# The last product in two column halves, one of the last multiplications on GpSimd, and the order and size of the last stores

## The chip, the cores and the metric

The kernel runs on one core of one Trainium2 chip. The metric is the device time of one execution in microseconds (us), as the median of several executions. A core has five engines that run side by side and wait for each other through semaphores: TensorE (PE in the profile, its weight loads PEld), VectorE (DVE), ScalarE (ACT), GpSimd (POOL) and SyncE (SP, which here only issues transfers). A "q" behind an engine's name in the profile means its sequencer, the part that issues its instructions, waits, branches and starts transfers.

## The reference

```
batch, m, k, n = 16, 512, 1024, 768
y1 = np.matmul(x, w1)          # x (16, 512, 1024), w1 and w2 (1024, 768)
y2 = np.matmul(x, w2)
return (np.tanh(y1) * y2).astype(np.float32)
```

So 8192 rows of x, in 64 row tiles of 128, are multiplied by two weight matrices, and every output element is the tanh of one product times the other product.

## The kernel before

**Tiling.** The 64 row tiles fall into a head of 4, computed with plain matmuls while the weights are still landing, and 20 triples of three row tiles (`i` from 0 to 19). The 2 x 768 weight columns are three blocks of 512: `a` is `w1[:, :512]`, `b` is `w2[:, :512]`, and `g` holds `w1[:, 512:]` in its first 256 columns and `w2[:, 512:]` in its last 256. The inner dimension of 1024 is two halves of four 128-row steps. For one triple this is a product of a 3 x 2 block matrix with a 2 x 3 block matrix, 18 block products; the kernel forms sums of blocks (`A_SUMS` on x, `B_SUMS` on the weights) and needs 15, `p0` to `p14`. Each is four matmuls of 128x128 by 128x512 that accumulate in one PSUM bank (`product`, L440 to L443).

**What goes around the products.** `C_OPS` lists, for one triple, the products and what combines them: `copy` and `seed` (ACT copies a bank to SBUF or into another bank), `add` (DVE adds or subtracts a bank and an SBUF tile), `t` and `th` (ACT's tanh, of 512 columns or of the 256 columns of `w1` in block `g`, into an output tile `o`), `m` and `mh` (DVE multiplies that output tile by the other product, in place, 512 or 256 columns wide). The number behind `t`, `th`, `m`, `mh` is the row tile of the triple. The entries that matter here, near the end of the list, are

```
("seed16", "seed", ("add52",), "c9", "c1", -1),
("p2", "p", ("seed16",), "c9", 4, 6, False),
("m1", "m", ("p2", "t1"), 1, "c9", 1),
("p3", "p", ("add52", "seed16"), "c1", 8, 48, False),
("add4", "add", ("copy56", "p3"), "c8", "c1", "s56", (-1, 1)),
("th0", "th", ("add4",), 0, "c8", 1),
("mh0", "mh", ("add4", "th0"), 0, "c8", 1),
("th1", "th", ("p3",), 1, "c1", 1),
("mh1", "mh", ("p3", "th1"), 1, "c1", 1),
```

`c0` to `c10` are PSUM banks. So `p3` completes bank `c1`, which both `add4` (DVE) and `th1` (ACT) read, and `p2` completes bank `c9`, which `m1` reads. Where two engines touch one PSUM bank, the framework puts a semaphore between them, in the order in which the program names them.

**Order.** A planner (class `Planner`) lays all operations out in advance: each has an engine, an estimated duration, a due time, what it needs, and what it must only stay behind. The products have a fixed order (`plan.strict`, from `PE_ORDER`, and for the last triple `LAST_ORDER = "0 13 4 5 3 2"`); everything else takes the free slot that the planner finds, by due time when it has a choice. The planned start times give one program order (`sorted`, a stable sort, so that equal starts keep the order of the list), and each engine's queue runs its share of it strictly in order. `LATENCY` in the planner is what it reckons from the end of an operation to its use on another engine.

**The end of the program.** One piece of the head is held back: block `g` of row tile 3, eight matmuls `m3g0` to `m3g7` on a kept copy of that tile (L426), which the planner puts into gaps of TensorE during the last triple. Their due time is 10000 and more, so that they, their tanh `thg3` (L429) and their multiplication `mug3` (L433) give way to everything else. The output tiles of the last triple are rows 61, 62 and 63; each is stored in two parts, columns 0 to 511 and 512 to 767, by SP (L423), in the order in which the planner finds them done. Behind the last operation every engine reads a flag (L734; it says whether the inputs were in the range that the fast path takes, and is complete some 19 us before the end), branches over the general path (L735), drains and meets the others in a barrier (L828), for which SP first waits for every transfer.

GpSimd starts the loads of x with a cast to fp16 (L358) and runs a tiny copy in front of most of them, which makes it wait for an earlier transpose (L479). Its last load is that of row tile 63.

Of the kernel before, what the change touches and what calls it, by code (L numbers as in the profile page):

```python
# [9 lines left out]
ALU = mybir.AluOpType  # L10
# [60 lines left out]
LAST_ORDER = "0 13 4 5 3 2"  # L71


class Planner:
# [9 lines left out]
    def op(self, name, engines, due, needs, fn, *args, behind=(), issued=(), chains=(), xfer=0.0, latency=None, seeds=False,  # L84
           lands=None, hold=0.0):
        assert name not in self.ops, name
        self.ops[name] = dict(engines=engines, due=due, needs=[n for n in needs if n], behind=[n for n in behind if n], issued=[n for n in issued if n], fn=fn, args=args,
                              chains=chains, xfer=xfer, latency=latency, seeds=seeds, lands=lands, hold=hold)
        for c in chains:
            self.chains.setdefault(c, {"left": 0, "bank": None, "end": 0.0})["left"] += 1  # L90
# [149 lines left out]
def kernel(  # L240
# [7 lines left out]
    nc = tc.nc  # L248
    P = 128
    B, M, K = x.shape  # L250
    _, N = w1.shape
    KO = K // P
    KH = KO // 2
    MT = B * M // P
    F = 512
    G = N - F
    HEAD = 4
    TRIPLES = (MT - HEAD) // 3
# [7 lines left out]
    bf16, f16, f32, i32 = mybir.dt.bfloat16, mybir.dt.float16, mybir.dt.float32, mybir.dt.int32  # L266
# [8 lines left out]
    once = fast.enter_context(tc.tile_pool(name="once", bufs=1))  # L275
# [13 lines left out]
    wsum = {v: once.tile([P, KH, F], f16, name=f"b{v}") for v, *_ in B_SUMS}  # L289

    S_NAMES = [o[3] for o in C_OPS if o[1] in ("copy", "add") and o[3][0] == "s"]
    arena = once.tile([P, len(S_NAMES) * C_BUFS * F], f32, name="arena")
    SLOTS = len(S_NAMES) * C_BUFS
    c_bufs = {(s, j): arena[:, (n * C_BUFS + j) * F:(n * C_BUFS + j + 1) * F]
# [19 lines left out]
    op = plan.op  # L314
# [87 lines left out]
    def w_rhs(v, k):  # L402
        return w_block(v, slice(k, k + 1))[:, 0, :]
# [6 lines left out]
    def x_operand(i, v):  # L410
        if v & (v - 1):
            return s_bufs[v, i % S_BUFS]
        bit = v.bit_length() - 1
        return xt(HEAD + 3 * i + bit // 2)[:, bit % 2 * KH:(bit % 2 + 1) * KH, :]
# [4 lines left out]
    def out_tile(mt):  # L419
        return o_bufs[mt if mt < HEAD else HEAD + (mt - HEAD) % O_BUFS]  # L420
# [14 lines left out]
    def place(i, name):  # L435
        if name[0] == "c":
            return bank((i, name))
        return c_bufs[name, i % C_BUFS]

    def product(e, i, dst, a, b, begins):  # L440
        for k in range(KH):
            pin(nc.tensor.matmul(place(i, dst), x_operand(i, a)[:, k, :], w_rhs(b, k),  # L442
                                 start=begins and k == 0, stop=k == KH - 1, skip_group_check=True))  # L443

    def c_copy(e, i, dst, src, sign):
# [12 lines left out]
    def c_mul(e, i, r, src, lo, n, at):  # L458
        o = out_tile(HEAD + 3 * i + r)[:, lo:lo + n]
        pin(nc.vector.tensor_tensor(o, o, place(i, src)[:, at:at + n], ALU.mult))  # L460

    def flag_1(e):
        pin(nc.vector.tensor_scalar(good, sums, HIGH, None, ALU.is_le))
# [33 lines left out]
        position["p" + p, TRIPLES - 1] = TRIPLES * 15 + n  # L497
    sequence = sorted((z, i, p) for (p, i), z in position.items())
    slot_of = {(i, p): ORIGIN + z * SLOT for z, i, p in sequence}
    plan.strict = [f"{p}.{i}" for _, i, p in sequence]  # L500

    XW, XX = 0.655, 1.4
    on_sp = "x00 x10 x20 x30 x01 x11 a4 a5 x21 a6 x31 a7".split() + [f"g{k}{t}" for k in range(KH) for t in range(2)]
# [60 lines left out]
    def plain(mt, s, due, behind=()):  # L564
        for n, k in enumerate([k for u, k in slices if u == s]):
            before = list(behind) + ([f"m{mt}{s}0"] if n else [])
            op(f"m{mt}{s}{k}", {"pe": MM}, due(n), [f"c{s}{k}", f"e{mt}{k // KH}"], mm, (s, mt), mt, k, w_cols(s, k), n == 0,
               behind=before, chains=[(s, mt)])
        last = [f"m{mt}{s}{k}" for k in range(KO)]
        xt_readers[mt] += last  # L570
        return last
# [6 lines left out]
    def finals(mt, s, due, last):  # L578
        if s != "b":
            lo, n = (0, F) if s == "a" else (F, G)  # L580
            op(f"th{s}{mt}", {"act": 0.5 if n == F else 0.28}, due, last, plain_tanh, mt, lo, n, (s, mt), 0,
               behind=reuse_out(mt), chains=[(s, mt)])
        if s != "a":
            lo, n, at = (0, F, 0) if s == "b" else (F, G, G)
            op(f"mu{s}{mt}", {"dve": 0.6 if n == F else 0.33}, due, last + [f"th{'a' if s == 'b' else s}{mt}"], plain_mul, mt, lo, n,
               (s, mt), at, chains=[(s, mt)])
            outs[mt].insert(0 if s == "b" else 1, f"mu{s}{mt}")

    for n, s in enumerate("agb"):
        for mt in range(HEAD):  # L590
            if (s, mt) == ("g", HEAD - 1):
                due, behind = (lambda n: 1e4 + n), [f"p0.{TRIPLES - 1}"]
            else:
                due, behind = (lambda n: landed[slices["agb".index(s) * KO + n]] + 0.8 + 0.02 * mt), []
            finals(mt, s, due(KO - 1) + (5.0, 3.0, 4.0)[n], plain(mt, s, due, behind))

    c_ops = {o[0]: o for o in C_OPS}
    readers = {}
# [40 lines left out]
    for i in range(TRIPLES):  # L639
        for name, kind, needs, *_ in C_OPS:  # L640
            soonest[i, name] = max([until[i, n] for n in needs] + ([slot_of[i, name]] if kind == "p" else []))
            until[i, name] = soonest[i, name] + TIME[kind] + 0.2
        for v, a, b, how in A_SUMS:
            op(f"S{v}.{i}", {"dve": 0.335}, None, x_needs(i, a) + x_needs(i, b), x_sum, i, v, a, b, how,
               hold=needed(i, v) - S_AHEAD if i > 1 else 0.0,
               behind=[f"{r}.{i - S_BUFS}" for r in a_readers[v]] if i >= S_BUFS else first_done)
            for u in (a, b):
                if not u & (u - 1):
                    xt_readers[HEAD + 3 * i + (u.bit_length() - 1) // 2].append(f"S{v}.{i}")
        for o in C_OPS:  # L650
            name, kind, needs = o[:3]
            needs = [f"{n}.{i}" for n in needs]
            chains = sorted({(i, p) for p in o[3:6] if isinstance(p, str) and p[0] == "c"})
            if kind == "p":
                needs += x_needs(i, o[4]) + w_needs(o[5], 0) + w_needs(o[5], 1)
                op(f"{name}.{i}", {"pe": SLOT}, slot_of[i, name], needs, product, i, *o[3:], chains=chains)
                if not o[4] & (o[4] - 1):
                    xt_readers[HEAD + 3 * i + (o[4].bit_length() - 1) // 2].append(f"{name}.{i}")
                continue
            if kind in ("seed", "copy", "add"):  # L660
                before = []
                if o[3][0] == "s":
                    before = [f"{r}.{i - C_BUFS}" for r in readers[o[3]]] if i >= C_BUFS else all_casts
                if kind == "add":
                    op(f"{name}.{i}", {"dve": 0.6}, None, needs, c_add, i, *o[3:], behind=before, chains=chains, seeds=True)
                else:
                    op(f"{name}.{i}", {"act": 0.495}, None, needs, c_copy, i, *o[3:], behind=before, chains=chains, seeds=True)
                continue
            r = o[3]
            mt = HEAD + 3 * i + r  # L670
            due = soonest[i, name] + LAST
            if kind in ("t", "th"):
                lo, n = (0, F) if kind == "t" else (F, G)
                op(f"{name}.{i}", {"act": 0.5 if n == F else 0.285}, due, needs, c_tanh, i, r, o[4], lo, n, o[5],
                   behind=reuse_out(mt), chains=chains)
            else:
                lo, n, at = (0, F, 0) if kind == "m" else (F, G, G)
                op(f"{name}.{i}", {"dve": 0.6 if n == F else 0.335}, due + 1, needs, c_mul, i, r, o[4], lo, n, at, chains=chains)
                outs[mt].insert(0 if kind == "m" else 1, f"{name}.{i}")
    for mt in range(MT):  # L680
        i = (mt - HEAD) // 3 if mt >= HEAD else -1
        if mt < HEAD:
            n = F if mt == HEAD - 1 else N
            op(f"st{mt}", {"sp": 0.05}, 1e3, outs[mt][:1] if mt == HEAD - 1 else outs[mt], store, mt, 0, n, behind=[f"p12.{4 + mt}"], xfer=1.0)
            if n < N:
                op(f"st{mt}M", {"sp": 0.05}, 2e4, outs[mt][1:], store, mt, n, N - n, xfer=0.4)
            continue
        late = [f"{('p0', 'p4', 'p12')[(mt - HEAD) % 3]}.{i + 1}"] if i < TRIPLES - 2 else []
        if i == TRIPLES - 1:
            for a, lo, n in ((0, 0, F), (1, F, G)):  # L690
                part = outs[mt][a:a + 1]
                op(f"st{mt}{a}", {"sp": 0.05}, 2e4, part, store, mt, lo, n, xfer=0.4)
        else:
            op(f"st{mt}", {"sp": 0.05}, slot_of[max(i, 0), "p2"] + 12, outs[mt], store, mt, behind=late, xfer=1.0)
# [138 lines left out]
```

## Time and profile before

| what | us |
|---|---|
| median of 3 runs (lowest, highest) | 303.63 (303.56, 304.0) |
| span of the profiled execution, first to last instruction | 303.7 |
| device time noted for the profiled execution, with what lies around the span | 305.48 |
| TensorE busy | 291.2 (96%) |
| VectorE busy | 254.0 (84%) |
| ScalarE busy | 224.5 (74%) |
| GpSimd busy | 49.6 (16%) |
| last matmul ends | 298.1 |
| last VectorE instruction ends | 299.65 |
| last store: issued, landed | 299.77, 302.56 |

The span counts from the first to the last instruction of the program. Times of instructions are given from the start of the span. In the timeline a row is one instruction or several alike in a row (x3): its start, its length, the engine, the line of the kernel, the operation, what it writes and reads; in brackets how long the engine stood idle before it, and what ended that. Back-to-back instructions of one engine overlap a little, so that a row of three is shorter than three times one.

### The profile page before, as it was taken

The numbers are of one execution on the slowest core, as the hardware profiler recorded it, in microseconds if no ns is written. First come the engines' busy times: TensorE is split into PE (matmuls) and PEld (weight loads), VectorE is DVE, ScalarE is ACT, GpSimd is POOL, SyncE is SP. The second block draws the span as 40 slices with busy tenths as digits, with TensorE's granted clock in tenths as the row PEclk, the third lists the DMA queues.
The fourth block names the chain that finished last, engine by engine and source line by source line (L and its number), as shares of the span: only waits on it lengthen the run. The fifth ranks groups of instructions, "written<-read, shape, count | busy, mean of one in ns | idle before, by whom it ended". The sixth has DMA issues, their size and how long they took to land.

```text
span 303.7 us, 4640 instructions
## 1 busy us (share of the span) xinstructions
PE 291.2 (96%) x1377; PEld 133.3 (44%) x1377; DVE 254.0 (84%) x530; ACT 224.5 (74%) x451; POOL 49.6 (16%) x128
## 2 busy tenths in 40 slices
PE   8989989999999999999998999999999999999992
PEld 5435434444444444444443444444444444444440
DVE  1639999999797898978959898898989889898773
ACT  2687897688877988789787888767787767776542
POOL 0054032130301210212112111211121210000000
PEclk9999999999999999999999999999999999999999
DMA  7999999999999999999999999999999999131242
GB/s 232 385 290 208 169 124 144 175 203 236 187 158 222 190 276 281 154 205 277 210 225 241 238 245 230 249 254 190 254 280 164 299 246 253 77 155 52 104 190 92
DMA packets 84283, 63.51 MB, mean 209 GB/s; under 512 B 62752, under 2 KB 66336, under 8 KB 84256
## 3 DMA queue, kind: packets, MB, share of 16 engines
q1 hardware_dynamic: 73888, 45.36, 63.1%
q0 software_dynamic: 9792, 16.78, 38.2%
q10 hardware_dynamic: 576, 1.05, 1.0%
q8 instruction: 11, 0.18, 0.2%
q14 instruction: 16, 0.13, 0.2%
HBM read 39.85 MB, written 25.17 MB: 214 GB/s over the span
## 4 chain that ended last, share of the span: by engine, by line
PE 59%; DMA 26%; DVE 8%; ACT 2%; issue 2%; SPq 1%; ACTq 0%; POOL 0%; DVEq 0%; POOLq 0%
PE bank L442 55%; DMA xT<-xh 13%; DMA xh<-in_x_dram 7%; DMA arena<-in_w_dram 4%; PE bank L426 3%; DVE bank L452 3%; DVE o L460 2%; DVE early_x L417 2%; DMA wh<-in_w_dram 2%; ACT o L455 1%; ACT junk L386 1%; DVE arena L452 1%; PE bank L376 0%; ACTq L353 0%; DVE b L408 0%
## 5 line engine op out<-in xcount | busy, mean ns | idle before, releaser
L442 PE MATMUL bank<-b,early_x 128*128 128x512 f16 x640 | 148.4, 379 | 0.8 <-DVE arena L452 0.4
L442 PEld LDWEIGHTS <-early_x 128*128 128x128 f16 x800 | 78.1, 98 | 97.0 <-issue 3.4
L446 ACT ACTIVATE arena<-bank 128x512 f32<-128x512 f32 x100 | 58.7, 595 | 27.9 <-PE bank L442 27.8
L452 DVE TENSOR_TENSOR bank<-bank,arena 128x512 f32<-128x512 f32 x100 | 69.3, 694 | 10.5 <-ACT arena L446 4.2
L460 DVE TENSOR_TENSOR o<-o,bank 128x256 f32<-128x256 f32 (+1 forms) x120 | 63.1, 550 | 11.3 <-ACT o L455 9.9
L386 ACT ACTIVATE junk<-xh 128x1024 f16<-128x1024 f16 x60 | 63.3, 1055 | 0.3
L442 PEld LDWEIGHTS <-xT 128*128 128x128 f16 x400 | 38.9, 98 | 49.8 <-issue 4.0
L442 PE MATMUL bank<-b,xT 128*128 128x512 f16 x240 | 58.3, 379 | 0.0
L455 ACT ACTIVATE o<-bank 128x256 f32<-128x256 f32 x80 | 34.5, 437 | 18.2 <-DVE bank L452 15.8
L442 PE MATMUL bank<-wh,xT 128*128 128x512 f16 x160 | 40.9, 379 | 2.0 <-DVE bank L452 1.6
L442 PE MATMUL bank<-wh,early_x 128*128 128x512 f16 x160 | 41.0, 379 | 1.1 <-ACT bank L446 1.1
L358 POOL DMA_DIRECT2D xh<-in_x_dram x60 | 31.7, 528 | 35.4 <-PE bank L442 9.5
L479 POOL CAST held<-xT 128x1 f32<-128x1 f16 x53 | 12.8, 242 | 148.4 <-DMA xT<-xh 148.3
L417 DVE TENSOR_TENSOR early_x<-early_x,xT 128x512 f16<-128x512 f16 x80 | 31.8, 417 | 1.0 <-ACT xT L362 0.3
L446 ACT ACTIVATE bank<-bank 128x512 f32<-128x512 f32 x40 | 22.0, 579 | 11.0 <-PE bank L442 9.2
L455 ACT ACTIVATE o<-arena 128x512 f32<-128x512 f32 x40 | 25.1, 629 | 4.5 <-DVE arena L452 4.5
L426 PE MATMUL bank<-wh,xT 128*128 128x512 f16 x72 | 19.5, 379 | 1.5 <-DMA wh<-in_w_dram 0.9
L417 DVE TENSOR_TENSOR early_x<-xT,early_x 128x512 f16<-128x512 f16 x40 | 16.7, 417 | 5.0 <-DMA xT<-xh 5.0
L417 DVE TENSOR_TENSOR early_x<-xT,xT 128x512 f16<-128x512 f16 x40 | 16.7, 417 | 0.0
L452 DVE TENSOR_TENSOR bank<-arena,bank 128x512 f32<-128x512 f32 x20 | 13.8, 692 | 1.4 <-ACT o L455 1.3
L452 DVE TENSOR_TENSOR arena<-bank,arena 128x512 f32<-128x512 f32 x20 | 13.6, 679 | 0.0
L452 DVE TENSOR_TENSOR arena<-arena,bank 128x512 f32<-128x512 f32 x20 | 13.5, 677 | 0.0
(47 smaller groups left out, 133.8 us busy)
## 6 DMA issues: line engine op xcount, KB each, us to landing
out_dram<-o SPq DMA_DIRECT2D x60, 384.0 KB, 6.0
xh<-in_x_dram POOLq DMA_DIRECT2D x60, 256.0 KB, 7.1
arena<-in_w_dram SPq DMA_DIRECT2D x12, 256.0 KB, 5.5
early_x<-in_x_dram SPq DMA_DIRECT2D x8, 256.0 KB, 5.1
arena<-in_w_dram ACTq DMA_DIRECT2D x4, 256.0 KB, 5.9
wh<-in_w_dram POOLq DMA_DIRECT2D x8, 128.0 KB, 5.7
out_dram<-o SPq DMA_DIRECT2D x4, 256.0 KB, 2.5
xT<-xh SPq DMA_TRANSPOSE x57, 7.4
```

The lines of the kernel that those rows point to most:

```text
L358: pin(nc.gpsimd.dma_start(xh(mt), xf[mt]))
L386: pin(nc.scalar.activation(junk[:, :src.shape[-1]], src, ACT.Abs, scale=scale, accum_out=sums[:, column:column + 1]))
L417: pin(engine[e].tensor_tensor(x_operand(i, v), x_operand(i, a), x_operand(i, b), OP[how]))
L426: pin(nc.tensor.matmul(bank(chain), xt(mt)[:, k, :], rhs, start=first, stop=k == KO - 1, skip_group_check=True))
L442: pin(nc.tensor.matmul(place(i, dst), x_operand(i, a)[:, k, :], w_rhs(b, k), start=begins and k == 0, stop=k == KH - 1, skip_group_check=T ...
L446: pin(nc.scalar.activation(place(i, dst), place(i, src), ACT.Copy, scale=float(sign)))
L452: pin(nc.vector.tensor_tensor(place(i, dst), a, b, ALU.add if signs == (1, 1) else ALU.subtract))
L455: pin(nc.scalar.activation(out_tile(HEAD + 3 * i + r)[:, lo:lo + n], place(i, src)[:, :n], ACT.Tanh, scale=float(sign)))
L460: pin(nc.vector.tensor_tensor(o, o, place(i, src)[:, at:at + n], ALU.mult))
L479: pin(nc.gpsimd.tensor_copy(held, xt(mt)[:, 0, :1]))
```

## The change

- The last product of the last triple, `p2` of triple 19, is issued as two operations: columns 0 to 255 (`p2.19`, four matmuls) and columns 256 to 511 (`p2+.19`, four more with the same four weight loads again). Its multiplication `m1.19` becomes two of 256 columns, `m1.19` and `m1+.19`.
- The multiplication `mh1.19` moves from DVE to GpSimd. As GpSimd works on SBUF, ACT first copies the 256 columns from the bank into a new tile `apart` (`g1.19`).
- The tanh and the multiplication of the held-back rest get the due time of `p5` of the last triple in place of 10000 and more.
- Row tile 62 is stored in three parts of 256 columns: `m1`, `m1+`, `mh1`. The last triple's other two row tiles are stored in two parts as before.

```
+    apart = once.tile([P, G], f32, name="apart")
...
-    def product(e, i, dst, a, b, begins):
+    def product(e, i, dst, a, b, begins, lo=0, n=F):
         for k in range(KH):
-            pin(nc.tensor.matmul(place(i, dst), x_operand(i, a)[:, k, :], w_rhs(b, k),
+            pin(nc.tensor.matmul(place(i, dst)[:, lo:lo + n], x_operand(i, a)[:, k, :], w_rhs(b, k)[:, lo:lo + n],
                                  start=begins and k == 0, stop=k == KH - 1, skip_group_check=True))
...
+    def c_out(e, i, src):
+        pin(nc.scalar.copy(apart, place(i, src)[:, G:]))
+
+    def c_mul_out(e, i, r):
+        o = out_tile(HEAD + 3 * i + r)[:, F:]
+        pin(nc.gpsimd.tensor_tensor(o, o, apart, ALU.mult))
...
-    plan.strict = [f"{p}.{i}" for _, i, p in sequence]
+    HALVED = "p" + LAST_ORDER.split()[-1]
+    plan.strict = [f"{p}.{i}" for _, i, p in sequence] + [f"{HALVED}+.{TRIPLES - 1}"]
...
-            finals(mt, s, due(KO - 1) + (5.0, 3.0, 4.0)[n], plain(mt, s, due, behind))
+            finals(mt, s, slot_of[TRIPLES - 1, "p5"] if behind else due(KO - 1) + (5.0, 3.0, 4.0)[n], plain(mt, s, due, behind))
...
+                if (i, name) == (TRIPLES - 1, HALVED):
+                    op(f"{name}.{i}", {"pe": SLOT / 2}, slot_of[i, name], needs, product, i, *o[3:], 0, G, chains=chains)
+                    op(f"{name}+.{i}", {"pe": SLOT / 2}, slot_of[i, name], needs + [f"{name}.{i}"], product, i, *o[3:], G, G, chains=chains)
...
+                if (i, name) == (TRIPLES - 1, "m1"):
+                    for n, part in enumerate(("", "+")):
+                        op(f"{name}{part}.{i}", {"dve": 0.335}, due, needs + ([f"{HALVED}+.{i}"] if n else []), c_mul, i, r, o[4], n * G, G, n * G,
+                           chains=chains)
+                    continue
...
+                if (i, name) == (TRIPLES - 1, "mh1"):
+                    op(f"g1.{i}", {"act": 0.29}, due, needs, c_out, i, o[4], chains=chains)
+                    op(f"{name}.{i}", {"pool": 0.8}, due + 1, needs + [f"g1.{i}"], c_mul_out, i, r)
+                    outs[mt].insert(1, f"{name}.{i}")
+                    continue
...
-            for a, lo, n in ((0, 0, F), (1, F, G)):
-                part = outs[mt][a:a + 1]
+            done = outs[mt]
+            parts = [(done[:1], 0, F), (done[1:], F, G)]
+            if (mt - HEAD) % 3 == 1:
+                parts = [([f"m1.{i}"], 0, G), ([f"m1+.{i}"], G, G), (done, F, G)]
+            for a, (part, lo, n) in enumerate(parts):
                 op(f"st{mt}{a}", {"sp": 0.05}, 2e4, part, store, mt, lo, n, xfer=0.4)
```

More of the change, by code (lines that the diff above doesn't have):

```diff
@@ L655 @@
                 needs += x_needs(i, o[4]) + w_needs(o[5], 0) + w_needs(o[5], 1)
-                op(f"{name}.{i}", {"pe": SLOT}, slot_of[i, name], needs, product, i, *o[3:], chains=chains)
+                if (i, name) == (TRIPLES - 1, HALVED):
+                    op(f"{name}.{i}", {"pe": SLOT / 2}, slot_of[i, name], needs, product, i, *o[3:], 0, G, chains=chains)
+                    op(f"{name}+.{i}", {"pe": SLOT / 2}, slot_of[i, name], needs + [f"{name}.{i}"], product, i, *o[3:], G, G, chains=chains)
+                else:
+                    op(f"{name}.{i}", {"pe": SLOT}, slot_of[i, name], needs, product, i, *o[3:], chains=chains)
                 if not o[4] & (o[4] - 1):
```

## The prediction

> **What bounds the kernel now.** I read the page's busy shares first (PE 96% of the span, so only the two ends of the program are not TensorE's), then the timeline of the last 8 us, then what each engine does behind its last operation. The diff touches the last triple alone; nothing before 290 us has a new need or a new due time, so the sum is made for the last 8 us and added to the span.
>
> ```profile
> 296.19 0.63 ACT L455 ACTIVATE o<-arena 128x512 f32<-128x512 f32 x1
> 296.72 0.36 ACT L429 ACTIVATE o<-bank 128x256 f32<-128x256 f32 x1
> 297.29 0.38 ACT L455 ACTIVATE o<-bank 128x256 f32<-128x256 f32 x1 [0.20 <-PE bank L442]
> 298.44 0.38 ACT L455 ACTIVATE o<-bank 128x256 f32<-128x256 f32 x1 [0.76 <-DVE bank L452]
> ...
> 297.12 0.42 DVE L433 TENSOR_TENSOR o<-o,bank 128x256 f32<-128x256 f32 x1 [0.97 <-ACT o L429]
> 297.71 0.70 DVE L452 TENSOR_TENSOR bank<-arena,bank 128x512 f32<-128x512 f32 x1 [0.17 <-ACT o L455]
> 298.31 1.34 DVE L460 TENSOR_TENSOR o<-o,bank 128x256 f32<-128x256 f32 x3
> ...
> 299.77 0.91 SPq L423 DMA_DIRECT2D out_dram<-o  x1
> ```
>
> In order, ACT runs t1, thg3, th1, th0; DVE runs mug3, add4, then mh1, m1, mh0 as one row that ends at 299.65. add4 starts not when p3 is done (297.25, when th1 starts) but when th1 is through: both read bank c1. SP's last issue is at 299.77, lands 2.8 us later, and the span ends 1.1 us after that. This is the chain that the change works on. The other one, which it does not mention, is GpSimd's:
>
> ```profile
> 245.40 0.18 POOL L479 CAST held<-xT 128x1 f32<-128x1 f16 x1 [1.69 <-DMA xT<-xh]
> 249.04 0.53 POOL L358 DMA_DIRECT2D xh<-in_x_dram  x1 [3.46 <-ACT o L455]
> ```
> ```profile
> L828 SPq EVENT_SEMAPHORE  x14: 17/28/28, 301.7 to 303.6; - x14
> L828 POOLq EVENT_SEMAPHORE  x4: 17/17/17, 302.9 to 303.6; - x4
> L828 POOLq DRAIN  x3: 45/107/5614, 285.8 to 303.4; - x3
> ...
> L828 PEldq DRAIN  x2: 8/40/72, 298.7 to 303.2; - x2
> L828 ACTq DRAIN  x2: 8/46/83, 299.6 to 303.1; - x2
> L828 DVEq DRAIN  x2: 10/38/65, 300.3 to 303.2; - x2
> ```
>
> (Columns of this last view: count, then shortest/median/longest in ns, first and last start.) GpSimd's last work ends at 249.6. It reads the flag at 285.0, branches, and its first drain, at 285.79, lasts **5.614 us**, to 291.40, where every other engine's takes under 0.1. It had been idle for 36 us, so the drain waits for no row of this profile: I read the 5.6 us as the price of GpSimd's first drain after its loads. Today it is over 11.5 us before the barrier meets at 302.92 and costs nothing.
>
> **The change, part by part.**
>
> *Held-back tanh first.* In the planner thg3 is ready 0.18 after t1; with the early due time it is let through first, and t1 follows. On the chip thg3 can start when m3g7 is done (last of seven steps of 0.216, ends 296.27): 296.29 to 296.66, then t1 to about 297.28. t1 is wanted by m1 alone, at 297.9 or later, which hides the swap; without that cover it would cost t1's delay, some 0.4. mug3 moves from 297.12 to 296.70, so DVE is free at 297.1, before p3. Now add4 and th1 get equal planned starts (p3's end plus 0.2; before, mug3 held DVE 0.15 beyond that, and th1 came first). Equal starts keep list order: add4 goes first, at 297.29 in place of 297.71, **0.42 earlier**, and th1 waits for it (the same bank), to 297.29 + 0.70 + 0.02 = 298.01. That two readers of one bank run one after the other is a row of the trace:
>
> ```profile
> 291.49 0.60 ACT L455 ACTIVATE o<-bank 128x512 f32<-128x512 f32 x1 [0.27 <-PE bank L442]
> ...
> 292.12 0.70 DVE L452 TENSOR_TENSOR bank<-bank,arena 128x512 f32<-128x512 f32 x1 [1.03 <-ACT o L455]
> ```
>
> There t0 and add60 read c0, equal in plan, t0 first in the list, and DVE stood 1.03 us.
>
> *Copy g1.* One more ACT instruction, behind th1 and ahead of th0: priced as the 128x256 rows, 0.38, back-to-back starts 0.26 to 0.28 apart in the trace's pairs. th1 298.01, g1 298.28 to 298.66, th0 298.55 to 298.93 (298.82 before): th0 loses 0.11, and mh0 waits for it.
>
> *p2 in halves.* Eight matmuls of 256 columns for four of 512, with four more weight loads of 98 ns. The five 128x256 matmuls at L340 took 0.71 us with an end of 0.27, a step of 0.11; 8 x 0.11 = 0.88 against 4 x 0.216 = 0.86: +0.02, p2 whole at 298.14. The first half is there at about 297.7; m1 may start on it, or wait for the bank to be finished, 298.16. DVE starts its next operation 0.6 after add4, at 297.89, so the halves are worth 0 to 0.27 to m1; I take 0, as the two rows above say one engine per bank.
>
> *DVE.* m1 in two costs 0.33 + 0.33 for 0.60, +0.06; mh1 leaves, -0.33. m1 298.16, m1+ 298.49, mh0 when th0 is done, 298.96 to 299.37: **0.28 earlier** than 299.65.
>
> *GpSimd's multiplication.* No row shows it. Below: DVE's 128x256 multiplication, 0.42. Above: the 128x128 select on GpSimd, 0.287, counted wholly as per-element cost and doubled for two inputs: 0.287 x 2 x 2 = 1.15. The nearest reading takes the 0.184 of a 128x1 copy as fixed and (0.287 - 0.184)/127 = 0.8 ns per element and input: 0.184 + 256 x 2 x 0.8 = 0.6; I take 0.65. From the Trainium skill, GPSIMD Engine Reference, section Performance versus the Vector engine: a two-input operation costs about 2.6 cycles an element; an estimate by that page is 256 x 2.6 / 1.2 GHz = 0.55 and would end the sum 0.1 earlier. It starts behind g1, 298.72, and ends at 299.37. Behind it on GpSimd stand its flag read, its branch and its drain, and for these the barrier.
>
> *Stores.* Ten issues for nine; the new order is row 3's rest, m1, m1+, mh0, mh1. The last two issue at 299.40 and, 0.425 behind (the distance of 299.35 and 299.77), at 299.83: +0.05 to the last issue, but with 128 KB parts ahead of it instead of a 256 KB one. The last issue of before took 0.91 instead of the 0.33 of its neighbours, so it may take either.
>
> *The drain.* GpSimd's sequencer starts the flag read as the multiplication is released (0.485), and the drain 0.30 after the read's end, as at 285.49 to 285.79: 298.72 + 0.49 + 0.30 = 299.5, just past the multiplication's end. 299.5 + 5.61 = 305.1. From GpSimd's semaphore at 302.92 to the end of the span is 0.75; so **305.1 + 0.03 + 0.75 = 305.9**, 2.2 above 303.7, and everything won in the tail lies under it. The span is 0.07 above the median of the runs, so the forecast for the median is **305.8**. Its own bounds: 305.1 where th1 stays ahead of add4 (copy 0.72 earlier); 306.3 with 1.15 for the multiplication, 306.6 with the spread of the runs (0.4).
>
> **Rivals.**
>
> *A. The drain is not paid again, and the tail decides: faster.* The 5.6 us may belong to the idle time before it or be taken off by the multiplication; the three other POOL drains take 0.05 to 0.18. It matters only if longer than 302.9 - 299.5 = 3.4. Then SP sets the end: from its last issue's end (300.68) to the span's end 2.98, of which 0.33 was waiting for the landing. 299.83 + 0.33 + 2.65 = 302.8; with the long issue 303.4. Middle **303.1**. For: DVE ends 0.28 earlier. Against: 5.614 follows 36 idle us, so nothing was left to wait for. The Trainium skill, VectorE: DVE Perf Modes, section The DRAIN you can't avoid, has the drains before and after a program at about 12 ns, constant, on all five engines. By that rule the end would be this rival's; the 5614 here differs from it.
>
> *B. No change.* As A, but th1 and g1 behind add4 and the fifth issue give back what add4 gained: last issue 299.83 with 0.91 and the old landing time 2.8 ends at 299.83 + 2.8 + 1.1 = 303.7, **303.6** as a median.
>
> *C. The first multiplication on GpSimd itself pays such a price*: 5.6 more before its store. 299.37 + 5.6 = 305.0, store and end 3.9 later: **308.9**. Against: the select at 1.02 and the first copy on GpSimd paid nothing visible. The Trainium skill, GPSIMD Engine Reference, section Instruction dispatch, gives about 6 us, with no instruction in the profile, to the first call of a freshly loaded routine; no row here shows one.
>
> **How the numbers follow.** Drain behind the multiplication 0.74 (305.8, own range 305.1 to 306.6); A 0.12; B 0.10; C 0.04. A is faster by over 0.2% (0.6 us, about what a measurement here can tell from no change), B within it, the other two slower: 0.12, 0.10, 0.78. The range 303.0 to 306.6 leaves out C, a third of A and the ends of the forecast's own bounds, some 0.15 in all.
>
> **What would show it.** A POOL drain of some 5.6 us that starts near 299.5 and ends at 305; SP and the others waiting in the barrier behind it; add4 ahead of th1 at 297.3; mh0 ending near 299.4; m1 no earlier than p2+. It is wrong if the drain behind the multiplication is below 3.4 us.

## The result, and the profile after

| | before | changed kernel |
|---|---|---|
| device time, median of 4 runs each (us) | 303.75 (303.56 to 304.0) | 307.06 (306.06 to 307.84) |
| ratio, 95% interval | | 1.0108 (1.0083 to 1.0134): slower by 1.1% |
| span and device time of the profiled execution | 303.7, 305.48 | 304.2, 306.06 |
| `p3`'s first matmul starts | 296.23 | 294.52 |
| from there to the end of the span, "the tail" | 7.47 | 9.72 |
| last VectorE instruction ends | 299.65 | 297.70 |
| GpSimd's first drain at the end | 285.79 to 291.40 | 297.80 to 303.42 |

The change makes the kernel slower, by the mechanism that was forecast, and by more than was forecast. `p3`'s first matmul is a good place to lay the two traces over each other, since nothing behind it depends on the body of the program; "p3+3.2" below means 3.2 us after it, and "the tail" is the time from it to the end of the span. Its row (the matmuls of `p3` and of `p2` together) before and after:

```profile
296.23 1.89 PE L442 MATMUL bank<-b,xT 128*128 128x512 f16 x8
```
```profile
294.52 1.90 PE L443 MATMUL bank<-b,xT 128*128 128x512 f16 x12
```

Now and then an execution is some 6 or 7 us longer than the others of its kernel (the highest times of shift and tanh_only below, and one of the kernel before beside them); the ratios leave these out.

The profiled execution is the fastest of the four. Its page, busy shares:

```profile
span 304.2 us, 4655 instructions
...
PE 290.6 (96%) x1381; PEld 133.1 (44%) x1381; DVE 254.6 (84%) x530; ACT 224.6 (74%) x452; POOL 50.3 (17%) x129
```

Nothing in the shares shows where 2 us went: a drain isn't counted as busy. The timeline of the last microseconds, ACT, DVE and GpSimd:

```profile
294.60 0.38 ACT L430 ACTIVATE o<-bank 128x256 f32<-128x256 f32 x1
294.88 0.62 ACT L456 ACTIVATE o<-arena 128x512 f32<-128x512 f32 x1
296.31 0.38 ACT L456 ACTIVATE o<-bank 128x256 f32<-128x256 f32 x1 [0.82 <-DVE bank L453]
296.60 0.37 ACT L464 COPY apart<-bank 128x256 f32<-128x256 f32 x1
296.85 0.40 ACT L456 ACTIVATE o<-bank 128x256 f32<-128x256 f32 x1
...
295.01 0.42 DVE L434 TENSOR_TENSOR o<-o,bank 128x256 f32<-128x256 f32 x1 [0.57 <-ACT o L430]
295.58 0.70 DVE L453 TENSOR_TENSOR bank<-arena,bank 128x512 f32<-128x512 f32 x1
296.51 1.19 DVE L461 TENSOR_TENSOR o<-o,bank 128x256 f32<-128x256 f32 x3 [0.23 <-PEq L761]
...
297.05 0.73 POOL L468 TENSOR_TENSOR o<-o,apart 128x256 f32<-128x256 f32 x1 [43.66 <-ACT apart L464]
```

The order is the one that the prediction derived: thg3 ahead of t1, add4 at p3+1.06 with th1 behind it at p3+1.79, then g1 and th0. DVE's last three are m1, m1+ and mh0 (p3+1.99 to p3+3.18; before, its last ended at p3+3.42). So VectorE's work in the tail does end 0.24 earlier. The L461 row names "PEq L761" as what released m1: TensorE's sequencer going on behind the last matmul, that is the end of the second half `p2+`. Now the end-of-program barrier, with count, shortest/median/longest in ns, first and last start:

```profile
L854 SPq EVENT_SEMAPHORE  x14: 17/28/28, 299.8 to 304.2; - x14
L854 POOLq EVENT_SEMAPHORE  x4: 17/17/17, 303.5 to 304.1; - x4
L854 POOLq DRAIN  x3: 45/107/5614, 297.8 to 304.0; - x3
L854 SPq DRAIN  x3: 7/7/13, 301.2 to 303.7; - x3
...
L854 DVEq DRAIN  x2: 10/44/77, 298.7 to 303.7; - x2
```

GpSimd's drain has the same 5614 ns as before, but it now begins behind the multiplication. SP, which has waited for every store, drains at 301.2 and is at the barrier at 301.30 (p3+6.78; before p3+6.66). GpSimd arrives at 303.5. The others wait 2.1 us for it, and the span ends 0.75 later.

The Trainium skill, VectorE: DVE Perf Modes, section The DRAIN you can't avoid, puts the drains that the runtime adds before and after a program at some 12 ns on all five engines. The drains here stand on a line of the kernel, so that the page may not mean them. SP's 7 to 13 ns are near its figure; GpSimd's 5614 is not, and here it is what the change costs.

### The profile page after: what moved, and what is told of

Its sections match the earlier page's. It is cut to its first block, busy times and chain, and to the rows that moved or that the text cites. A ratio compares the mean times of both kernels' runs of the same rounds, so it can differ in the third digit from the quotient of the medians.

```text
span 304.2 us, 4655 instructions
## 1 busy us (share of the span) xinstructions
PE 290.6 (96%) x1381; PEld 133.1 (44%) x1381; DVE 254.6 (84%) x530; ACT 224.6 (74%) x452; POOL 50.3 (17%) x129
## 3 DMA queue, kind: packets, MB, share of 16 engines
q0 software_dynamic: 9792, 16.78, 37.1%
## 5 line engine op out<-in xcount | busy, mean ns | idle before, releaser
L461 DVE TENSOR_TENSOR o<-o,bank 128x256 f32<-128x256 f32 (+1 forms) x120 | 63.1, 549 | 13.6 <-ACT o L456 11.7
L443 PE MATMUL bank<-b,xT 128*128 128x512 f16 (+1 forms) x244 | 58.3, 375 | 0.0
```

The costliest lines, as they stand in the source:

```text
L443: pin(nc.tensor.matmul(place(i, dst)[:, lo:lo + n], x_operand(i, a)[:, k, :], w_rhs(b, k)[:, lo:lo + n], start=begins and k == 0, stop=k = ...
```

## The experiments

Each was timed against the kernel before on the same chip; "tail" is as above, from the run's own trace.

| run | median us (runs, range) | kernel before beside it | ratio, 95% | tail |
|---|---|---|---|---|
| early_drain | 303.74 (12, 303.29 to 304.52) | 304.04 | 0.9989 (0.9972 to 1.0007) | 7.34 |
| no_pool | 303.73 (12, 303.09 to 306.68) | 304.04 | 0.9998 (0.9976 to 1.0019) | 7.37 |
| pool_only | 306.9 (4, 306.01 to 309.92) | 304.04 | 1.0118 (1.0068 to 1.0168) | 9.86 |
| touch | 305.07 (10, 304.72 to 308.75) | 304.04 | 1.0047 (1.0018 to 1.0077) | 8.83 |
| again | 305.99 (8, 305.56 to 307.47) | 304.12 | 1.0055 (1.0022 to 1.0089) | 9.72 |
| shift | 303.69 (10, 303.06 to 311.02) | 304.12 | 0.9979 (0.9961 to 0.9998) | 7.53 |
| tanh_only | 304.26 (10, 303.73 to 309.84) | 304.12 | 0.9995 (0.9975 to 1.0015) | 7.44 |
| best | 303.96 (12, 303.61 to 304.57) | 304.12 | 0.999 (0.9975 to 1.0006) | 7.47 |
| mid_drain | 303.74 (10, 303.33 to 304.83) | 304.06 | 0.9978 (0.995 to 1.0006) | 7.74 |

**early_drain: the changed kernel with the drain paid where nobody waits.** One instruction more, behind GpSimd's last load of x:

```
         ...                                  # load_x, behind the cast of the load
+        if mt == MT - 1:
+            pin(nc.gpsimd.drain())
```

> The change, with one more instruction: GpSimd drains right behind its last load, at about 250 us, where it has nothing else to do. Theory (the drain that comes first behind GpSimd's loads costs 5.6 us, once): a drain of 5 us or more near 250, the last one at about 0.1 us, and the end set by SP again, which in the changed kernel's profile stood in the barrier at 301.3 and waited 2.1 us for GpSimd: 306.1 - 2.1, so 303.5 to 304.2 against 303.6 to 303.9 before. Rival 1 (every drain at the end behind a multiplication on GpSimd is long): no gain, 306 to 307.8. Rival 2 (of the 3.3 us only 2.2 are the drain's; the rest is lost in the body through the new tile or the new order): about 304.8 to 305.

The added drain (line L361 of this kernel), and GpSimd's at the end (L856):

```profile
L361 POOLq DRAIN  x1: 6898/6898/6898, 247.6 to 247.6; - x1
```
```profile
L856 POOLq DRAIN  x3: 39/41/107, 298.1 to 301.9; - x3
```

With everything else of the change in place, the 5.6 us at the end are 0.04 and the tail falls from 9.72 to 7.34. The time is the kernel before's again: that drain is the whole cost of the change that lasts from run to run. And with it gone, the rest of the change leaves 0.13 us in the tail, less than the 0.6 that a measurement of this kernel can tell.

**no_pool: the change without its GpSimd part.** mh1 stays on DVE, no g1; halves, tanh and smaller stores stay.

```
-                if (i, name) == (TRIPLES - 1, "mh1"):
-                    op(f"g1.{i}", ...
-                    op(f"{name}.{i}", {"pool": 0.8}, ...
```

> The change without its GpSimd part: the last product in halves, the held-back rest's tanh first and the smaller stores stay, that multiplication is back on VectorE and the copy is gone. Theory: GpSimd's drain lies at 285 as before and costs nothing; add4 starts 0.4 us earlier, so 303.0 to 303.8 against 303.6 to 303.9 before. Rival (the halves or the stores cost something themselves): 304.5 or more.

```profile
L849 POOLq DRAIN  x3: 45/107/5614, 284.1 to 301.6; - x3
```

GpSimd is free again, its drain starts at 284.1 and is over long before anybody waits: tail 7.37, time as before. Halves, tanh and stores together take 0.1 us off the tail. That is no more than two traces of the same instructions differ by (before and shift 7.47 and 7.53; in the changed kernel's two traces SP reaches the barrier 0.24 apart), so a gain is not shown.

**pool_only: the GpSimd part alone, on the kernel before.**

```
+                if (i, name) == (TRIPLES - 1, "mh1"):
+                    op(f"g1.{i}", {"act": 0.29}, due, needs, c_out, i, o[4], chains=chains)
+                    op(f"{name}.{i}", {"pool": 0.8}, due + 1, needs + [f"g1.{i}"], c_mul_out, i, r)
+                    continue
...                                           # the tile apart, c_out, c_mul_out; mh1's store waits for GpSimd
```

> The kernel before with the GpSimd part alone: copy by ScalarE, multiplication on GpSimd. Theory: th1 ends at 297.67 of the old timeline, the copy at 297.95, the multiplication runs 298.0 to 298.75, the drain starts there and lasts 5.6, so the end is 298.8 + 5.6 + 0.8 = 305.2 for 303.7, 1.5 us slower. Rival (the loss needs the other parts): within 0.6 of before.

```profile
L840 POOLq DRAIN  x3: 45/113/5616, 299.0 to 305.2; - x3
```

The loss is there with this part alone, and larger than expected (306.9 for 305.2). The tail, 9.86, is 2.39 longer than before: the drain begins at p3+3.41. The expectation had it 0.84 earlier, because it let the copy g1 start as soon as th1 was through; in the trace the copy waits another 0.76 for add4, which reads the same bank and comes ahead of it. Of the 2.86 between the medians that leaves 0.5 to the body. This trace, of the execution of 307.22, shows TensorE waiting 0.89 behind a late transposed tile, which the trace of the changed kernel does not, and 0.62 at another place where that one has 0.40. Such waits are the subject of the section on the prediction.

**touch: GpSimd woken late for nothing.** A copy of one column on GpSimd, which waits for th1 of the last triple and whose result nobody reads, added to the kernel before:

```
+    def touch(e, i):
+        pin(nc.gpsimd.tensor_copy(held, out_tile(HEAD + 3 * i + 1)[:, F:F + 1]))
...
+    op("touch", {"pool": 0.1}, 1e4, [f"th1.{TRIPLES - 1}"], touch, TRIPLES - 1)
```

> The kernel before with one tiny copy on GpSimd (128x1) that waits for th1 of the last triple and whose result nobody reads. Theory: it only makes GpSimd's drain late: released at 297.7, flag read 0.5, drain near 298.5 and 5.6 long, end 298.5 + 5.6 + 0.8 = 304.9 for 303.7, 1.2 us slower. Rival (the multiplication's length, its copy or its late store cost the time): no change, within 0.3.

```profile
295.86 0.18 POOL L463 COPY held<-o 128x1 f32<-128x1 f32 x1 [48.25 <-ACT o L455]
```
```profile
L832 POOLq DRAIN  x3: 45/107/5614, 296.7 to 302.8; - x3
```

Here no multiplication moved, no store waits for GpSimd, and the kernel is still slower: the tail grows by 1.35 where 1.2 was expected (the drain begins at p3+2.38 and lasts 5.61, and 0.83 lies behind it). So it is not GpSimd's multiplication, its speed or its store that costs, but that any late instruction on GpSimd holds back the drain behind it.

**again and shift: the changed kernel once more, and the kernel before with everything in memory 1 KB higher.** "again" has no edit; "shift" adds only the tile that the change adds, unused:

```
+    apart = once.tile([P, G], f32, name="apart")
```

> The changed kernel once more, in more rounds. From the start of the last triple's p3 to the end its profile took 9.72 us, the kernel before 7.47: 2.25 more, all of it GpSimd's drain. Theory: that is the whole loss, and the first four times (306.06 to 307.84) had also caught waits in the body, which come and go in every kernel here (the profile of before had two of them, 0.46 and 1.16 us): 2.2 to 2.6 us over before, 306.0 to 306.7. Rival (1 us more is lost in the body, through the new tile or the order): 3.0 or more over before again.

> The kernel before with the new tile allocated and unused, so that every tile behind it lies 1 KB higher in each partition. Theory: no effect, within 0.4 us of before. Rival (the shifted addresses cost 1 us in the body): 304.7 to 305.

The changed kernel's eight new runs have a median of 305.99, its trace the same drain and the same tail as the first:

```profile
L854 POOLq DRAIN  x3: 45/113/5616, 297.7 to 303.9; - x3
```

The eight runs are 1.87 above the kernel before beside them, less than the 2.2 to 2.6 expected; the interval of the ratio, 0.7 to 2.7 us, holds the 2.25 of the tail. Over all twelve runs of it the median is 306.25, with four at 307.2 to 307.8. "shift" has the instructions of before and came out at 0.9979, with an interval that just leaves out 1: I take two parts in a thousand for noise in this comparison. A loss of 1 us through the place of the tiles, the rival, is out.

**tanh_only: the new due time of the held-back rest alone.**

```
-            finals(mt, s, due(KO - 1) + (5.0, 3.0, 4.0)[n], plain(...))
+            finals(mt, s, slot_of[TRIPLES - 1, "p5"] if behind else due(KO - 1) + (5.0, 3.0, 4.0)[n], plain(...))
```

> The kernel before with only the new due time of the held-back rest's tanh and multiplication. Expected: add4 ahead of th1 and 0.4 us earlier than before, measured from p3, but th1 then waits for it and VectorE's mh1, first in its queue, waits for th1: add4 to 1.66 behind p3's start, th1 to 2.2, mh1, m1, mh0 end at 3.5 where before they end at 3.42. No gain, 0 to 0.2 us slower, not to be told from before by its time. Rival (the tanh first is what the change gains): mh0 ends 0.2 earlier and the tail from p3 to the end is below 7.3.

Its timeline, DVE:

```profile
295.49 0.70 DVE L452 TENSOR_TENSOR bank<-arena,bank 128x512 f32<-128x512 f32 x1 [0.15 <-PE bank L442]
296.64 1.35 DVE L460 TENSOR_TENSOR o<-o,bank 128x256 f32<-128x256 f32 x3 [0.45 <-ACT o L455]
```

add4 now waits for TensorE and not for th1, as intended (p3+1.06). But th1 comes behind add4, mh1 is first of DVE's last three and waits 0.45 for th1, and DVE ends at p3+3.56, 0.14 later than before. By itself, moving add4 ahead gains nothing that can be measured; where mh1 leaves DVE as well, DVE ends at p3+3.18 (after and best).

**best: the parts that help, with the drain paid early.** On the kernel before: mh1 on GpSimd from the copy, the new due time, the early drain; p2 whole and two stores for row tile 62.

```
+        if mt == MT - 1:
+            pin(nc.gpsimd.drain())
...                                           # and the edits of pool_only and tanh_only, whole
```

> The kernel before with the GpSimd multiplication, the tanh first, and GpSimd's drain right behind its last load; the last product whole and row tile 62 stored in two parts as before. Theory: the drain costs nothing at 250, and SP has one issue less behind the last work than the changed kernel (each took 0.48 there): the last issue some 3.7 us behind p3's start, tail 6.8 to 7.1 against 7.47: 0.3 to 0.6 us faster than before, 303.3 to 303.7. Rival (SP's and the stores' fixed end eats it): within 0.2.

```profile
L842 POOLq DRAIN  x3: 39/41/107, 297.7 to 301.6; - x3
```

The drain is out of the way, but the expected gain did not come: tail 7.47, the kernel before's. The last store is issued at p3+3.70 as reckoned and lands 2.63 later. With the 1.14 from its landing to the end of the span, the expected tail had left it 2.0 to 2.3: one small store by itself lands in 1.7 us, the last of several does not. SP reaches the barrier at p3+6.66, where it did before. No version here is measurably faster than the kernel before.

**Three small programs: what the drain is a price of.** They leave out the reference's computation. A tile is loaded, ACT is kept busy for some 20 us after the load, GpSimd multiplies 128x256, SP stores the result. They differ in who loads and how often:

```
pin((nc.gpsimd if BY_POOL else nc.sync).dma_start(loaded[j], xf[j]))   # LOADS times
...
pin(nc.gpsimd.tensor_tensor(o[:, 512:], o[:, 512:], junk[:, :256], ALU.mult))
pin(nc.sync.dma_start(of[0], o))
```

> A small program that leaves out the products and all but one output tile: one tile of x is loaded by SP, ScalarE copies for some 20 us, GpSimd makes one 128x256 multiplication of two SBUF tiles, SP stores one tile. Theory (the long drain is the price of GpSimd having issued DMAs): GpSimd's drain at the end lasts under 0.2 us. Rival (it is the price of GpSimd's arithmetic, or of its first drain in a program): about 5.6.

> The same program with the one load issued by GpSimd (with its cast), some 15 us or more before its drain. Theory: the price is fixed and paid once: 5.6 us. Rival (it grows with the number of loads; the kernel has 68, so 0.08 each): about 0.1.

> The same with sixteen loads by GpSimd. Theory: 5.6 us as with one. Rival (it grows with the loads): 1.3 us.

GpSimd's multiplication and the drains of the end, with the load on SP:

```profile
27.61 0.72 POOL L34 TENSOR_TENSOR o<-o,junk 128x256 f32<-128x256 f32 x1 [27.17 <-DVEq L61]
...
L61 POOLq DRAIN  x3: 34/70/827, 27.6 to 31.2; - x3
```

with one load on GpSimd:

```profile
28.39 0.72 POOL L34 TENSOR_TENSOR o<-o,junk 128x256 f32<-128x256 f32 x1 [26.46 <-DVE o L33]
...
L61 POOLq DRAIN  x3: 34/78/917, 28.4 to 32.1; - x3
```

and with sixteen:

```profile
48.40 0.72 POOL L34 TENSOR_TENSOR o<-o,junk 128x256 f32<-128x256 f32 x1 [32.78 <-DVE o L33]
...
L61 POOLq DRAIN  x3: 34/90/2147, 48.4 to 52.1; - x3
```

The drain begins with the multiplication here, so its first 0.72 us are the multiplication's. Behind that it lasts 0.07 without a load, 0.16 with one, 1.39 with sixteen. A price fixed per program, which was my theory, would have been 5.6 with one load as with sixteen: it falls. The slope is (1.39 - 0.16) / 15 = 0.082 us for each DMA that GpSimd has issued, and 68 x 0.082 = 5.6 is the drain of the kernel, which issues 68 loads on GpSimd. Eight of them, the weights, are half as large as the others. By size the price would be that of 64, 5.25, and the drain took 5.61: it goes by their number. (Each load here is 144 packets, large or small, 9792 in all in the page of before; whether it is the load or the packet that counts isn't told apart.)

**mid_drain: the same drain, but in the middle of the loads.** The changed kernel with its drain behind the load of row tile 37: 42 of the 68 loads lie before it, 26 behind.

```
-        if mt == MT - 1:
+        if mt == 37:
             pin(nc.gpsimd.drain())
```

> The changed kernel with a drain of GpSimd behind the load of row tile 37, that is behind 42 of its 68 loads; none behind the last. The small programs gave 0.07 us with no load, 0.16 with one, 1.39 with sixteen: 0.082 us for each load since the last drain. By that the drain in the middle takes 42 x 0.082 = 3.5 us and what its last loads still need, and the one at the end 26 x 0.082 + 0.05 = 2.2 us, from 3.3 to 5.5 behind p3's start, hidden behind SP's 6.5: tail 7.3 to 7.6, no slower than before unless the drain in the middle makes a load late. Theory it would refute (a fixed 5.6 once loads were issued): 5.6 at the end again, tail 9.7.

```profile
L361 POOLq DRAIN  x1: 10592/10592/10592, 140.8 to 140.8; - x1
...
L856 POOLq DRAIN  x1: 2177/2177/2177, 298.6 to 298.6; - x1
```

The last drain is 2.177 us where 26 x 0.082 + 0.05 = 2.2 was reckoned. So the price counts the loads since the drain before. The middle one missed its expectation: 10.6 us for 3.5 and what the transfer in flight adds. The load ahead of it, still in flight, landed at 149.6, and the drain ended 1.8 us behind that; what it does beyond the wait isn't settled. In early_drain, too, the drain (6.9) was longer than 68 x 0.082, and ended 2.8 behind its load's landing at 251.7. The tail of 7.74 is not the drain's: that was over at 300.8, and SP came at 302.2, behind the last store, which was issued at p3+3.83 and landed 2.82 later, at 302.0.

## Why the prediction was right, and where it was wrong

**Right: the mechanism, and its size.** A drain of 5.61 us starts behind the multiplication, ends last, and everything that the tail gains lies under it. The tail grew by 9.72 - 7.47 = 2.25; forecast 2.2. early_drain and no_pool each take the loss away, pool_only and touch each bring it about. Rival A (not paid again) falls with that. Rival C (the first multiplication pays itself) falls too: the multiplication took 0.73. Rival B, that the other edits give back what they gain, is what early_drain and no_pool show of the change without its drain (7.34 and 7.37 for 7.47).

**Wrong: the last term of the range, "306.6 with the spread of the runs (0.4)", and the step under it, "The span is 0.07 above the median of the runs".** The 0.4 was the spread of three runs. Measured, the twelve executions of the changed kernel go from 305.56 to 307.84, 2.3 us, and five of them lie above 306.6, three of these among the first four. The kernel before, in the executions beside the experiments that the ratios use, goes from 303.21 to 307.33. The prediction could have seen it. "0.07 above" set a span beside a device time. The profiled execution of before has a span of 303.7 and a device time of 305.48: 1.8 us lie around the span, in the other kernels' runs as well (306.06 and 304.2 after). Its device time was thus 1.85 above the median of 303.63, and the trace had the reason in it. TensorE's waits before, in the timeline of PE:

```profile
81.81 1.02 PE L442 MATMUL bank<-wh,xT 128*128 128x512 f16 x4 [0.46 <-DVE bank L452]
...
160.82 1.02 PE L442 MATMUL bank<-wh,xT 128*128 128x512 f16 x4 [1.16 <-DVE bank L452]
```

DVE was itself late there, waiting for a transposed tile of x. The same two stretches, by windows (stretch, its length, then busy time of PE, PEld, DVE, ACT, POOL; granted clock, DMA share, GB/s), before:

```profile
70.00:90.00 20.00, 19.54 (x91) 8.67 (x90) 17.62 (x38) 15.55 (x32) 3.12 (x8) 1.00 1.16 195
...
150.00:170.00 20.00, 18.84 (x88) 8.45 (x87) 16.50 (x36) 15.18 (x32) 3.85 (x10) 1.00 1.18 234
```

and after:

```profile
70.00:90.00 20.00, 20.00 (x94) 9.05 (x93) 18.73 (x40) 16.16 (x35) 4.22 (x10) 1.00 1.19 244
...
150.00:170.00 20.00, 20.00 (x94) 9.11 (x93) 17.02 (x37) 16.42 (x35) 3.67 (x10) 1.00 1.16 221
```

TensorE is busy for 19.54 and 18.84 of 20 us before, for 20.00 in both after: 0.46 + 1.16 = 1.62 us of such waits, by which `p3` started later in the profile of before (296.23 against 294.52, 1.71). They come and go from one execution to the next; pool_only's trace has one in the first of these stretches (0.89), after's has none. Two things follow for the numbers. In the centre the error cancelled, as the baseline's waits stand on both sides of the difference: 303.63 + 2.2 is 305.8, which is what the fastest of the four runs, 306.06, and the eight of "again", 305.99, came to. But the range was too narrow above: an execution with such waits is some 1.6 us longer, as the very profile that I summed on was, so the forecast's own upper end had to be about 306.6 - 0.4 + 1.8 = 308.0, not 306.6. The first four runs' median, 307.06, lies there. That those runs had such waits isn't shown: only the fastest of the four has a trace, and the spans of the others (304.9, 306.1, 305.6) say only that the excess is inside the program. Why the first four runs' median is 1 us above that of the eight later ones stays open.

**Right in its place, wrong as a reading: "the price of GpSimd's first drain after its loads".** 5.61 was right because the change does not alter the 68 loads. As a fixed price it would mislead elsewhere: it is 0.082 per load since the last drain.

**The smaller steps.**

| step | predicted | measured |
|---|---|---|
| add4, th1 start | p3+1.06, p3+1.78 | p3+1.06, p3+1.79 |
| halves of p2, worth to m1 | 0 | 0 |
| mh0 ends | p3+3.14 | p3+3.18 |
| GpSimd's multiplication | 0.65 (0.42 to 1.15) | 0.73 |
| drain starts | p3+3.27 | p3+3.28 |
| last store issued | p3+3.60 | p3+3.83 |

The halves: m1's first half needs only columns that were done 0.4 us earlier, and yet waited. In the view of line L461, from 295 to 298 us, DVE's sequencer:

```profile
L461 DVEq EVENT_SEMAPHORE  x2: 21/446/870, 295.6 to 296.6; - x2
```

One of these two waits is of 870 ns and lasts until `p2+` is through (296.42); m1 starts at 296.51. So the wait guards the bank as a whole. The Trainium skill, PSUM — Partial Sum Buffer, section PSUM bank collisions raise a hardware error, asks for just that, also for disjoint columns of one bank; and here the halves of one bank did not bring the first multiplication forward.

The last store came 0.23 later than reckoned. mh0 ended 0.04 later; its store was issued 0.16 behind its end where the sum had put 0.03, though the row of before has 0.12; and the last issue stands 0.49 behind that one, not 0.425. An issue on SP took 0.39 here for the last three stores, where most of those in the profile before took 0.33. The view of the store's line, from 294 to 300 us:

```profile
L424 SPq DMA_DIRECT2D out_dram<-o x5: 332/390/393, 295.5 to 298.4; - x5
...
DMA to landing us min/median/max: 1.7/2.6/2.8
```

Nor do smaller parts land sooner: the first two land in 1.7 us, the last three in 2.6 to 2.8, as the last one before did (2.79). So SP reaches the barrier at p3+6.78 in this trace, 0.12 later than before, though DVE ends 0.24 earlier. In the trace of "again" the last store lands in 2.43 and SP is there at p3+6.54, 0.12 earlier than before: this difference is one of executions.

Three numbers of the prediction's working don't hold, and none moves the forecast. Its lower bound, "305.1 where th1 stays ahead of add4 (copy 0.72 earlier)", is the case of pool_only, and there the copy is not earlier: it waits for add4, and the drain starts at p3+3.41, 0.13 later than in the changed kernel. In rival A, from the end of SP's last issue to the end of the span it is 3.02, not 2.98. And 305.8 with 0.5 for the multiplication and 0.4 for the spread is 306.7, not 306.6.

## What to carry to other kernels

Before giving an idle engine late work, look at what its queue does at the end of the program: a drain or a release that hides behind 10 us of idleness becomes the path as soon as the engine's last instruction moves behind it, be it a copy of one column. If GpSimd has issued many transfers, an explicit drain where it stands idle takes their price off the end. And compare spans with spans and device times with device times; a profile whose device time lies above the runs may have waits in it, as this one had, which must be found before its length is a baseline. Three runs that lie close together don't give the spread of the next four.

## What the runs showed of the hardware, unexpected

- GpSimd's drain costs 0.082 us for each load that it issued since the drain before, also long after they have landed (32 us in the kernel before): 0.07 us with none, 0.16 with one, 1.39 with sixteen, 2.18 with twenty-six, 5.61 with sixty-eight.
- A drain right behind a load ended only after that load had landed, and lasted longer: 6.9 us in early_drain, 10.6 in mid_drain.
- A 128x256 f32 store landed 1.7 us after its issue when none or one that had nearly landed was ahead of it, 2.1 us (no_pool) to 3.2 (pool_only) with others just ahead; issues on SP that followed each other directly stood 0.43 to 0.49 us apart in the kernel before and the changed one.
